# A row of 1/rms by way of HBM instead of four transposes, in a two-layer encoder trunk on one core

## The chip, the core and the metric

One core of one Trainium2 chip. The metric is the device time of one execution in microseconds (us), lower is better. Engines go by the profile's names: PE (TensorE, matmuls), PEld (its weight loads), DVE (VectorE), ACT (ScalarE), POOL (GpSimd) and SP (SyncE, which here only issues DMAs).

## The reference

Two layers over one sequence of 512 tokens of width 1024, all in float32. In short:

```python
xn = rmsnorm(x, norm1_g)
u, q, k, v, g_a, g_b = split(xn @ w_in)          # u, v, g_a, g_b: 1024 wide; q, k: 4 heads x 2 x 128
q, k = rotary(rmsnorm(q)), rotary(rmsnorm(k))    # per head, first 32 of 128 entries turned
a = softmax(q0 k0) - lam * softmax(q1 k1)        # per head, chunk-causal with chunks of 64
o = rmsnorm(a @ v) * (1 - lam_init)
p = (windowed mean of u over 2, 4, 8, 16 tokens - u) @ w_pool * pool_scale
x = x + (sigmoid(g_a) * p + sigmoid(g_b) * o) @ w_out
x = x + swiglu(rmsnorm(x, norm2_g))              # hidden width 2816
```

rmsnorm(x) is x / sqrt(mean(x^2) + 1e-6) times a gain. The 1/rms is one number per token. It can therefore be applied after a product with `w_in`, which is what the kernel does.

## The kernel before, in words

**Products.** A float32 product is made of three matmuls of rounded parts: each operand is split in a high part (a cast on ACT, the first half of `split`, L213) and a low part (the difference, a subtraction on DVE, the second half). `product` (L303) then issues ah x bh, ah x bl and al x bh (L308, L309, L310) for each slice of the inner dimension. Names end in h and l (or hi and lo): xh, xl; qh, ql; vh, vl; uh, ul; and ah, al for the probabilities.

**Weights.** They come as 307 pieces of 512 KB in the order of `weight_plan` (L61). `loaded` (L220) requests a piece on SP's queue into one of seven buffers `raw` (L225) and notes the request in the list `transfers`.

**Round trips through HBM.** SP's queue also carries the kernel's block transposes: `turned` (L318) transposes within blocks on DVE (L323), writes the tile to HBM (`away<-near`, L324) and reads it back in another order (`near<-away`, four transfers, L328). A transfer on SP's queue that must wait holds everything behind it.

**Order of the work.** `clock` counts the columns that the matmuls have taken so far (a matmul of 512 columns adds 512, a transpose 256, L316). `later(delay, what)` (L261) puts a step into a heap, due `delay` columns from now, and `run_due` (L271), called ahead of every slice of a product, issues what has fallen due. So steps are written into the program between the matmuls at places that the counter sets, and the framework's scheduler makes each engine's order of that. Every engine works its instructions in order and waits where one is not ready.

**A layer's first half.** The heads are worked in the order 3, 2, 1, 0 (`attention`, L523). For each: the product for q and k (`evicted`, `rotated`, `turn`), and per block t of 128 tokens the scores (`scores`, L548, with a mask memset L558, a maximum on DVE L559 and the exponential on ACT L560), the difference of the two softmaxes, its transpose, the split into `ah` and `al` (`turn_prob`, L577), and the product with v (`weighted`, L596), whose result ACT squares (L604). The widest scores, of the last block, have 512 columns. v itself comes from a product whose result ACT and DVE evict into vh and vl (L691, L692).

`merged(j)` (L733) follows a head by one: it makes u and the gate g_a of group j. `windowed` (L709) multiplies u by the row of 1/rms on DVE (`up`, L714), adds shifted copies (`us`, L719), and finishes with three short steps (`head`, L722, L723, L725), after which u is split into uh and ul. For the gates, DVE multiplies the product by the row of 1/rms (`ta<-mm,hg`, L748), ACT takes the tanh (L752).

**The row of 1/rms.** `token_stats` (L429) makes 1/rms with tokens along the partitions: `stats[:, 1, :]`, 128 partitions x 4, by a pow on POOL (L440). `windowed` and the gates need it with tokens along the free dimension and the same in all 128 partitions: `rms_rows[layer]`, which is the second half of the tile `hg` (`head_gains`, L176; the first half holds rotary tables). `spread_rms` (L501) makes that row: it transposes each column of `stats`, broadcast to 128 x 128, on PE (L315) into one PSUM bank, and ACT copies the bank into `hg` (L506). It is queued by `later(81600, ...)` at the layer's start (L512). Its first reader is `up` of the first head's `merged`.

Of the kernel before, what the change touches and what calls it, by code (L numbers as in the profile page):

```python
# [10 lines left out]
F32 = mybir.dt.float32  # L11
# [7 lines left out]
P = 128  # L19
# [3 lines left out]
NT = S // P  # L23
# [31 lines left out]

QK_AWAY, SCORE_AWAY, PROB_AWAY, AV_AWAY, MERGE_AWAY = 28000, 26000, 32000, 18000, 24000
NORMED, ROTATED, JOINED, GATED, SUMMED, GATE = 7200, 2400, 2400, 4800, 9600, 2400
HIDDEN_DELAYS = (26000, 28000), (8000, 14000)


# [64 lines left out]
def trunk_kernel(  # L125
# [10 lines left out]
    nc = tc.nc  # L136
# [3 lines left out]
    hbm = ctx.enter_context(tc.tile_pool(name="hbm", bufs=1, space=bass.MemoryType.DRAM))  # L140
# [29 lines left out]
    rotary, rms_rows = {}, {}  # L170
# [5 lines left out]
    def head_gains(layer):  # L176

        g = sb.tile([P, 2, S], F32, name="hg", tag="hg")
        rms_rows[layer] = g[:, 1, :]
        cs, sn = rotary[layer] = [g[:, 0, i * VD:(i + 1) * VD].rearrange("p (a t r) -> p a t r", a=2, t=NT) for i in range(2)]  # L180
        row = sb.tile([P, 2, ROT], F32, name="gr", tag="m12")
        for a in range(2):
            nc.sync.dma_start(row[:, a, :], spread(rows[layer][R_QG + QK * a:R_QG + QK * a + ROT]))
        for a in range(2):
            def times(to, table, gains):
                nc.gpsimd.tensor_tensor(to, table, gains.unsqueeze(1).broadcast_to(list(table.shape)), op=ALU.mult)
            times(cs[:, a], cos_t, row[:, a, :])
            for h in range(2):
                here, there = slice(h * HALF, (h + 1) * HALF), slice((1 - h) * HALF, (2 - h) * HALF)
                times(sn[:, a, :, here], sin_t[:, :, here], row[:, a, there])  # L190
        nc.gpsimd.tensor_tensor(gain_column(layer, 0), gain_column(layer, 0), gain_column(layer, 1), op=ALU.mult)
        nc.gpsimd.memset(gain_column(layer, 0)[:ROT], 1.0)
# [16 lines left out]
    transfers = []  # L209

    def split(hi, lo, src):

        return nc.scalar.copy(hi, src), nc.vector.tensor_sub(lo, src, hi.bitcast(F32))  # L213
# [47 lines left out]
    def later(delay, what):  # L261
        heapq.heappush(waiting, (clock[0] + delay, count[0], what))
        count[0] += 1
# [50 lines left out]
    def transpose(dst, src):  # L314
        nc.tensor.transpose(dst, src, ident)  # L315
        clock[0] += 2 * P  # L316

    def turned(src, n, tag=None, bufs=1, near=None, wait=0):  # L318

        if near is None:  # L320
            near = sb.tile([P, n * P], F32, name="near", tag=tag, bufs=bufs)
        away = hbm.tile([P, n * P], F32, name="away", tag="away", bufs=8)
        nc.vector.transpose(near.rearrange("p (c k j) -> p k c j", c=4, k=n), src.rearrange("p (k c i) -> p k c i", k=n, c=4))  # L323
        nc.sync.dma_start(away, near)  # L324

        def back():
            for c in range(4):
                nc.sync.dma_start(  # L328
                    near[32 * c:32 * (c + 1), :].rearrange("i (q r) -> i q r", q=4),
                    away.rearrange("(q i) (c r) -> c i q r", q=4, c=4)[c])  # L330

        def back_behind():
            with tc.issue_after(transfers[-1].ins):
                back()

        if wait:
            later(wait, back_behind)
        else:
            back()
        return near.rearrange("p (q k j) -> p k q j", q=4, k=n)  # L340

    def squares_of(x):
        return x.rearrange("p k (q j) -> p k q j", q=4)
# [48 lines left out]
    def token(t):  # L392
        return slice(t * P, (t + 1) * P)
# [19 lines left out]
    stats = [None]  # L413
# [86 lines left out]

    def spread_rms(layer):  # L501

        row = tr_ps()
        for t in range(NT):
            transpose(row[:, token(t)], stats[0][:, 1, t:t + 1].broadcast_to([P, P]))
        nc.scalar.copy(rms_rows[layer], row)  # L506

    for layer in range(L):
        lam_init = 0.8 - 0.6 * math.exp(-0.3 * layer)
        if layer:  # L510
            head_gains(layer)
        later(81600, lambda layer=layer: spread_rms(layer))  # L512

        def x_tok(t):
            return [(xh[:, k, token(t)], xl[:, k, token(t)]) for k in range(KD)]
# [335 lines left out]
        class Hidden:  # L851
# [9 lines left out]
            def put(self, half, t, gate, up):  # L861
# [10 lines left out]
                if t:  # L872
                    back, done = HIDDEN_DELAYS[self.f0 >= GROUPS[-1] and self.f0 < ODD]
                    near = turned(h.rearrange("p i t c -> p (i t c)"), 4, ("up", "us")[half], 2, wait=back)
                    later(back + done, lambda: self.back(half, near))

            def back(self, half, near):

                with tc.issue_after(made[0].ins), tc.issue_after(made[1].ins):
                    split(*(squares_of(x[:, half].rearrange("p i c -> p (i c)").rearrange("p (k c) -> p k c", c=P))  # L880
                            for x in self.parts), near)
                ready.add((layer, self.f0, half))
# [222 lines left out]
```

## Time and profile before

| what | value |
|---|---|
| median of 3 runs | 1377.12 us (1376.54 to 1377.54) |
| the profiled execution | 1376.3 us, of it 1374.5 us span |
| PE busy | 1369.2 us (6238 matmuls and transposes) |
| DVE busy | 996.2 us |
| ACT busy | 775.5 us |
| POOL busy | 131.2 us |
| DMA | 224.07 MB, mean 163 GB/s |

The span goes from the first to the last instruction of the profiled execution. Busy times of an engine's instructions can overlap, since its pipeline starts one before the last has ended: for PE, the distance between two starts tells more than a duration does. A row of the timeline gives the start, the duration, the engine, the line, the operation with output and inputs, the shape, a count where several like ones stand together, and in brackets how long the engine was idle before it and for whom it waited.

### The profile page before, as it was taken

The page shows a single profiled execution, that of the slowest core. Times are in us where ns is not written, and L with a number is a line of the kernel's source. Part 1 is how long each engine was busy: PE and PEld are TensorE (multiplying, and loading weights), DVE is VectorE, ACT ScalarE, POOL GpSimd, SP SyncE. Part 2 cuts the span into 40 slices and gives each one's busy share as a digit, 9 for nine tenths or more (in the row PEclk, how much of TensorE's full clock was granted, in tenths as well). Part 3 has the DMA queues.
Part 4 walks back from the last instruction along what each step waited for, and adds up shares of the span by engine and source line. Part 5 has one row for each costly group of instructions (what it writes and reads, how often), then busy time and mean ns, then how long its engine had stood idle before and what let it go on. Part 6 is the DMA issues. An engine that isn't in the chain of part 4 may idle for free.

```text
span 1374.5 us, 18657 instructions
## 1 busy us (share of the span) xinstructions
PE 1369.2 (100%) x6238; PEld 1138.2 (83%) x6238; DVE 996.2 (72%) x1787; ACT 775.5 (56%) x1577; POOL 131.2 (10%) x155
## 2 busy tenths in 40 slices
PE   9999999999999999999999999999999999999999
PEld 7888888888888888888888888888888888888887
DVE  7668667687968768678666786765878687686782
ACT  7765554554757545554367755556557665555540
POOL 4010100000101101110010001010001111000100
PEclk9999999999999999999999999999999999999999
DMA  8244444444667968676435455444536788687831
GB/s 314 86 144 133 135 139 146 146 130 147 138 179 196 234 183 213 176 202 190 143 107 165 130 171 160 138 131 139 162 111 140 197 217 214 189 207 178 206 123 62
DMA packets 141072, 224.07 MB, mean 163 GB/s; under 512 B 41392, under 2 KB 88496, under 8 KB 140976
## 3 DMA queue, kind: packets, MB, share of 16 engines
q1 hardware_dynamic: 130464, 187.20, 42.7%
q0 software_dynamic: 9216, 33.56, 14.2%
q10 hardware_dynamic: 1296, 2.13, 0.6%
q8 instruction: 49, 0.80, 0.2%
q14 instruction: 47, 0.39, 0.1%
HBM read 193.59 MB, written 29.23 MB: 162 GB/s over the span
## 4 chain that ended last, share of the span: by engine, by line
PE 99%; DMA 0%; issue 0%; DVE 0%; ACT 0%; SPq 0%; ACTq 0%; DVEq 0%
PE mm L290 17%; PE mm L289 17%; PE mm L291 17%; PE mm L308 15%; PE mm L309 15%; PE mm L310 15%; PE mm L485 0%; PE mm L484 0%; PE mm L486 0%; PE mm L315 0%; PE mm L438 0%; DMA res<-in_x_t 0%; PE mm L493 0%; ACT ah L213 0%; DVE xh L473 0%
## 5 line engine op out<-in xcount | busy, mean ns | idle before, releaser
L213 DVE TENSOR_TENSOR wlo<-raw,whi 128x1024 fp32r<-128x1024 f32 (+1 forms) x220 | 266.8, 1217 | 75.7 <-ACT whi L213 74.9
L213 ACT CAST whi<-raw 128x1024 fp32r<-128x1024 f32 (+1 forms) x220 | 229.4, 1051 | 143.4 <-PE mm L291 75.0
L308 PE MATMUL mm<-whi,xh 128*128 128x512 f32 x480 | 188.8, 393 | 0.0
L310 PE MATMUL mm<-whi,xl 128*128 128x512 f32 x480 | 187.1, 390 | 0.0
L309 PE MATMUL mm<-wlo,xh 128*128 128x512 f32 x480 | 187.1, 390 | 0.0
L289 PE MATMUL mm<-whi,xh 128*128 128x512 f32 x384 | 149.6, 390 | 0.0
L291 PE MATMUL mm<-whi,xl 128*128 128x512 f32 x384 | 149.4, 389 | 0.0
L290 PE MATMUL mm<-wlo,xh 128*128 128x512 f32 x384 | 149.4, 389 | 0.0
L290 PE MATMUL mm<-fl,whi 128*128 128x512 f32 (+1 forms) x356 | 137.6, 387 | 0.0
L291 PE MATMUL mm<-fh,wlo 128*128 128x512 f32 (+1 forms) x356 | 137.6, 387 | 0.0
L289 PE MATMUL mm<-fh,whi 128*128 128x512 f32 (+1 forms) x356 | 137.6, 387 | 0.0
L767 DVE TENSOR_TENSOR res<-mm,res 128x512 f32<-128x512 f32 (+1 forms) x145 | 97.7, 678 | 44.0 <-PE mm L291 41.8
L353 POOL TENSOR_TENSOR r<-r,mhalf 128x4 f32<-128x4 f32 (+1 forms) x64 | 59.3, 929 | 512.0 <-DVE r L352 492.1
L239 POOL DMA_DIRECT2D wlo<-in_wts x64 | 56.1, 876 | 536.6 <-ACT wlo L238 363.0
L310 PEld LDWEIGHTS mm<-whi,xl 128*128 128x128 f32 x480 | 90.1, 188 | 19.2
L309 PEld LDWEIGHTS mm<-wlo,xh 128*128 128x128 f32 x480 | 90.3, 188 | 17.3
L308 PEld LDWEIGHTS mm<-whi,xh 128*128 128x128 f32 x480 | 90.2, 188 | 17.3
L308 PE MATMUL mm<-xh,whi 128*128 128x512 f32 x256 | 99.8, 390 | 0.0
L309 PE MATMUL mm<-xl,whi 128*128 128x512 f32 x256 | 99.8, 390 | 0.0
L310 PE MATMUL mm<-xh,wlo 128*128 128x512 f32 x256 | 99.6, 389 | 0.0
L291 PEld LDWEIGHTS mm<-whi,xl 128*128 128x128 f32 x384 | 72.1, 188 | 15.0
L290 PEld LDWEIGHTS mm<-wlo,xh 128*128 128x128 f32 x384 | 72.1, 188 | 15.0
(220 smaller groups left out, 2761.9 us busy)
## 6 DMA issues: line engine op xcount, KB each, us to landing
raw<-in_wts SPq DMA_DIRECT2D x243, 512.0 KB, 3.9
wlo<-in_wts POOLq DMA_DIRECT2D x64, 512.0 KB, 6.2
away<-near SPq DMA_DIRECT2D x73, 256.0 KB, 2.3
near<-away SPq DMA_DIRECT2D x292, 64.0 KB, 2.8
away<-near SPq DMA_DIRECT2D x29, 128.0 KB, 1.9
near<-away SPq DMA_DIRECT2D x116, 32.0 KB, 2.1
pwr<-in_pool_w ACTq DMA_DIRECT2D x8, 256.0 KB, 2.9
out<-res SPq DMA_DIRECT2D x7, 256.0 KB, 2.0
```

The source lines that it names most:

```text
L213: return nc.scalar.copy(hi, src), nc.vector.tensor_sub(lo, src, hi.bitcast(F32))
L239: nc.gpsimd.dma_start(lo.rearrange("p a b -> p (a b)"), wts[piece_no], accum_op=ALU.add)
L289: nc.tensor.matmul(acc, lhsT=ah, rhs=bh, start=start, stop=False, **check)
L290: nc.tensor.matmul(acc, lhsT=ah, rhs=bl, start=False, stop=False, **check)
L291: last = nc.tensor.matmul(acc, lhsT=al, rhs=bh, start=False, stop=stop, **check)
L308: nc.tensor.matmul(acc, lhsT=ah, rhs=bh, start=i == 0, stop=False)
L309: nc.tensor.matmul(acc, lhsT=ah, rhs=bl, start=False, stop=False)
L310: last = nc.tensor.matmul(acc, lhsT=al, rhs=bh, start=False, stop=i == n - 1)
L353: nc.gpsimd.tensor_tensor(r, r, mhalf[:, :width], op=ALU.pow)
L767: return nc.vector.tensor_add(res[d][:, cs], acc, res[d][:, cs])
```

## The change

`spread_rms` no longer uses PE and ACT. It takes a small buffer `row` in HBM (4 x 128 numbers), writes `stats[:, 1, :]` into it with one transfer on SP's queue (128 partitions x 4 numbers of 4 bytes, turned by the pattern of the destination), and queues a second transfer 36000 columns later, which reads the 512 numbers back, broadcast to 128 partitions, into `hg`. The second is tied in the program's order behind the newest request of weights (`transfers[-1]`). The first step is queued for 72000 columns instead of 81600. The four calls of `transpose` no longer add their 4 x 256 columns to `clock`.

```diff
+ROW_BACK = 36000
...
     def spread_rms(layer):
 
-        row = tr_ps()
-        for t in range(NT):
-            transpose(row[:, token(t)], stats[0][:, 1, t:t + 1].broadcast_to([P, P]))
-        nc.scalar.copy(rms_rows[layer], row)
+        row = hbm.tile([NT, P], F32, name="row", tag="row", bufs=2)
+        nc.sync.dma_start(row.rearrange("t p -> p t"), stats[0][:, 1, :])
+
+        def back():
+          with tc.issue_after(transfers[-1].ins):
+            nc.sync.dma_start(rms_rows[layer], row.rearrange("t p -> (t p)").partition_broadcast(P))
+
+        later(ROW_BACK, back)
 
     for layer in range(L):
...
-        later(81600, lambda layer=layer: spread_rms(layer))
+        later(72000, lambda layer=layer: spread_rms(layer))
```

In the rows that follow, line numbers of after are one higher up to `spread_rms` and five higher behind it, and buffer numbers differ; the tiles named before and after are the same ones.

SP's queue in layer 0, before: the first weights, two rows of parameters (`lv`), and the weights behind them.

```order
L225 DMA raw<-in_wts 128x1024 x4
L686 DMA lv<-in_rows 128x512 x2
L225 DMA raw<-in_wts 128x1024 x13
L324 DMA away<-near 128x512
L328 DMA near<-away 32x4x128 x4
```

The same place after.

```order
L226 DMA raw<-in_wts 128x1024 x4
L691 DMA lv<-in_rows 128x512 x2
L505 DMA row<-stats 128x4x1
L226 DMA raw<-in_wts 128x1024 x4
L509 DMA hg<-row 128x512
L226 DMA raw<-in_wts 128x1024 x9
```

The write of the row stands ahead of 13 requests of weights and the read ahead of 9. In layer 1 the two stand next to each other, behind nine requests of weights and ahead of two `away<-near` and eight `near<-away`.

PE in layer 1, around the third block of `weighted` of the second head (`mm_7930<-vh,ah`) and the first gate product of `merged` for group 2 (`mm_7891<-xh,whi`; `mm_7951` is the next gate product), before.

```order
L310 MATMUL mm_7891<-xh_6424,wlo_7722 128x512
L308 MATMUL mm_7930<-vh_7437,ah_7841 128x256
L309 MATMUL mm_7930<-vl_7438,ah_7841 128x256
L308 MATMUL mm_7951<-xh_6424,whi_7703 128x512
L309 MATMUL mm_7951<-xl_6425,whi_7703 128x512
L310 MATMUL mm_7951<-xh_6424,wlo_7704 128x512
L310 MATMUL mm_7930<-vh_7437,al_7842 128x256
```

The same place after (`mm_7885` is the gate product, `mm_7924` the block).

```order
L309 MATMUL mm_7885<-xh_6421,whi_7715 128x512
L310 MATMUL mm_7885<-xl_6422,whi_7715 128x512
L311 MATMUL mm_7885<-xh_6421,wlo_7716 128x512
L309 MATMUL mm_7924<-vh_7431,ah_7835 128x256
L310 MATMUL mm_7924<-vl_7432,ah_7835 128x256
L311 MATMUL mm_7924<-vh_7431,al_7836 128x256
```

The three matmuls of the next gate product no longer stand between the block's second and third matmul.

DVE at that place, before: the last steps of the window (`us`, `head`), the low part `al` of the block's probabilities, and `ta`, the gate product times the row.

```order
L719 TENSOR_TENSOR us_7884<-us_7881 128x512
L213 TENSOR_TENSOR al_7842<-pr_7641,ah_7841 128x384
L722 TENSOR_TENSOR head_7887<-us_7884,tab_68 128x16
L723 SCALAR_TENSOR_TENSOR us_7884<-us_7884,up_7872 128x496
L725 TENSOR_TENSOR us_7884<-head_7887,up_7872 128x16
L748 TENSOR_TENSOR ta_7949<-mm_7891,hg_6559 128x512
```

The same place after.

```order
L724 TENSOR_TENSOR us_7875<-us_7872 128x512
L753 TENSOR_TENSOR ta_7943<-mm_7885,hg_6556 128x512
L723 MEMSET us_7878 128x16
L724 TENSOR_TENSOR us_7878<-us_7875 128x512
L718 MEMSET up_8729 128x16
L727 TENSOR_TENSOR head_7881<-us_7878,tab_68 128x16
L728 SCALAR_TENSOR_TENSOR us_7878<-us_7878,up_7866 128x496
L730 TENSOR_TENSOR us_7878<-head_7881,up_7866 128x16
L723 MEMSET us_8732 128x16
L718 MEMSET up_8778 128x16
L214 TENSOR_TENSOR al_7836<-pr_7635,ah_7835 128x384
```

`ta` has moved ahead of the window's last step, and `al` behind all of the window. On ACT the cast of that block's `ah`, which stood ahead of the tanh of `ta` with two instructions between them, now stands directly behind it.

## The prediction

> **What bounds the kernel now.** I read the page first, then the list of waits on PE, then the timelines of the places that the change touches.
>
> ```profile
> span 1374.5 us, 18657 instructions
> PE 1369.2 (100%) x6238; PEld 1138.2 (83%) x6238; DVE 996.2 (72%) x1787; ACT 775.5 (56%) x1577; POOL 131.2 (10%) x155
> PE 99%; DMA 0%; issue 0%; DVE 0%; ACT 0%; SPq 0%; ACTq 0%; DVEq 0%
> ```
>
> ```profile
> PE mm L405 <- DVE us L718: 1.2, 1, 1.2
> PE mm L493 <- DVE xh L473: 0.6, 1, 0.6
> ```
>
> The third line is the chain that ended last: 99% of it is PE. The list of PE's waits has two rows, both at the start, 1.8 us in all. So there is one bound from end to end, and only two kinds of effect count: instructions that PE no longer has to do, and new moments in which PE has nothing it may start. The profiled execution took 1376.3 us (span 1374.5), 0.8 under the median of 1377.12, so I add the change's sum to both alike. A measurement of this kernel can tell about 0.2%, 2.75 us, from no change.
>
> **What it removes.** Per layer four transposes of the 1/rms column on PE and one copy on ACT.
>
> ```profile
> 53.10 0.60 PE L315 MATMUL mm<-ident,stats 128*128 128x128 f32 x4
> 53.45 0.42 PE L308 MATMUL mm<-qh 128*128 128x384 f32 x1
> ```
>
> ```profile
> 727.61 0.60 PE L315 MATMUL mm<-ident,stats 128*128 128x128 f32 x4
> 727.96 0.48 PE L308 MATMUL mm<-whi,xh 128*128 128x512 f32 x1
> 728.27 0.39 PE L309 MATMUL mm<-wlo,xh 128*128 128x512 f32 x1
> ```
>
> ```profile
> 729.86 0.57 ACT L506 COPY hg<-mm 128x512 f32<-128x512 f32 x1
> ```
>
> Durations of pipelined matmuls overlap, so I go by starts. The four transposes hold PE for 53.45 - 53.10 = 0.35 us, and again 0.35 in layer 1; the matmul behind them is followed after 0.31 (727.96 to 728.27), where two 512-column matmuls follow each other by 0.22 or 0.23 (807.20 and 807.42 further down), so another 0.08, which I take for layer 0 as well. That is 0.43 a layer, **-0.87 us** in all. The copy (0.57) goes from an engine that is 56% busy and is not on the chain: 0.
>
> **What it adds on SP.** Two transfers per layer, `row<-stats` and `hg<-row`, in the queue that carries the weights and the round trips. The first can't leave before POOL's pow has made 1/rms, the second not before the first has landed, and all that stands behind them on SP waits too.
>
> ```profile
> 22.43 2.01 POOL L440 TENSOR_TENSOR stats<-stats,mhalf 128x4 f32<-128x4 f32 x1
> ```
>
> ```profile
> 16.00 12.03 SPq L225 DMA_DIRECT2D raw<-in_wts  x7
> ```
>
> ```profile
> 30.66 2.01 ACT L213 CAST whi<-raw 128x1024 fp32r<-128x1024 f32 x2
> 33.64 0.47 ACT L691 ACTIVATE vh<-mm,stats 128x256 fp32r<-128x256 f32 x1 [0.97 <-PE mm L310]
> ```
>
> ```profile
> raw<-in_wts SPq DMA_DIRECT2D x243, 512.0 KB, 3.9
> near<-away SPq DMA_DIRECT2D x116, 32.0 KB, 2.1
> ```
>
> Layer 0: before, the weights behind `lv` were requested from 16.00 on. Now they stand behind `row`, which waits for the pow's end at 24.44: about 8.5 us later. They take 3.9 to land, so they are there at about 29, and the casts that read them stand at 30.66; ACT then still idles 0.97. Cover 1.5 us or more, cost 0. If it were gone, each microsecond would first eat that 0.97 of ACT.
>
> ```profile
> 693.35 0.33 SPq L225 DMA_DIRECT2D raw<-in_wts  x1
> 707.55 1.84 SPq L324 DMA_DIRECT2D away<-near  x2
> ```
>
> ```profile
> 702.02 1.04 POOL L440 TENSOR_TENSOR stats<-stats,mhalf 128x4 f32<-128x4 f32 x1 [54.49 <-DVE stats L439]
> ```
>
> ```profile
> 719.34 0.69 DVE L213 TENSOR_TENSOR ql<-near,qh 128x512 fp32r<-128x512 f32 x1 [1.80 <-ACT qh L213]
> ```
>
> ```profile
> 726.85 0.33 PE L308 MATMUL mm<-qh 128*128 128x256 f32 x1
> ```
>
> Layer 1: nothing stands between the two new transfers, so the delay of 36000 units that the code puts between them does not separate them in SP's queue. But SP has nothing to do from 693.68 to 707.55. `row` leaves when the pow ends at 703.06; the round trips are due at 707.55, 4.5 us later; and what they feed (`ql`, ready at 720.03) is wanted by PE at 726.85, another 6.8. Less some 0.9 for two issues, `row` may take 10.4 us to land before PE notices. The trace has no transfer of 512 pieces of 4 bytes. Below, it is bounded by a small round trip's 2.1 us; above, by four times that, 8.4, if pieces alone count (that transfer has 128 of them). Both lie under 10.4: cost 0, with the upper end as a rival below.
>
> **What it moves.** The four transposes advanced the counter of columns by 1024 units a layer, and everything queued by that counter now falls due at slightly other places; the orders in the section on the change show where this bites: layer 1, second head, third block of `weighted`. Before, that block's ah and al were cast early, the cast of `al` stood ahead of the window's last steps on DVE, and PE had three matmuls of the next gate product between the block's second and third matmul. After, the block comes directly behind the last matmul of the first gate product; on DVE `ta`, which waits for that matmul, stands ahead of a whole tail of the window and of `al`; on ACT the tanh of `ta` stands ahead of `ah`. So PE waits for a chain that begins with its own last result.
>
> ```profile
> 807.20 0.39 PE L310 MATMUL mm<-xh,wlo 128*128 128x512 f32 x1
> 807.42 0.28 PE L308 MATMUL mm<-vh,ah 128*128 128x256 f32 x1
> 807.54 0.28 PE L309 MATMUL mm<-vl,ah 128*128 128x256 f32 x1
> ```
>
> ```profile
> 793.41 0.11 DVE L558 MEMSET mm<- 64x64 f32 x1 [0.67 <-PE mm L310]
> 806.02 0.67 DVE L719 TENSOR_TENSOR us<-us 128x512 f32<-128x512 f32 x1
> 806.75 0.67 DVE L719 TENSOR_TENSOR us<-us 128x512 f32<-128x512 f32 x1
> 807.34 0.55 DVE L213 TENSOR_TENSOR al<-pr,ah 128x384 fp32r<-128x384 f32 x1
> 807.81 0.17 DVE L722 TENSOR_TENSOR head<-us,tab 128x16 f32<-128x16 f32 x1
> 808.57 0.68 DVE L748 TENSOR_TENSOR ta<-mm,hg 128x512 f32<-128x512 f32 x1
> ```
>
> ```profile
> 802.77 0.62 ACT L213 CAST uh<-us 128x512 fp32r<-128x512 f32 x1 [1.50 <-DVE us L725]
> 803.29 0.51 ACT L213 CAST ah<-pr 128x384 fp32r<-128x384 f32 x1
> 809.75 0.62 ACT L752 ACTIVATE ta<-ta 128x512 f32<-128x512 f32 x1
> ```
>
> In the clock of this trace, with PE 0.43 ahead in layer 1: PE would take the block at 807.42 - 0.43 = 806.99. `ta` can start when the gate product is out, 807.20 + 0.39 - 0.43 = 807.16, if DVE is free. But DVE works without a gap from 793.41, where the widest scores of the head start it, and those now come six 512-column matmuls later: 6 x 0.23 - 0.43 = 0.95 later. The step behind which `ta` now stands gave way at 806.75; with 0.95 that is **807.70**, which I take. Then: `ta` until 808.38 (0.68), tanh, and the cast of `ah` 0.52 behind it (802.77 to 803.29), done after 0.51: 809.41. PE has been idle for 2.4. Two matmuls 0.12 apart bring it to 809.65. On DVE behind `ta` stand one more `us` (0.59, 806.75 to 807.34), three short steps (0.76, 807.81 to 808.57), some 0.2 of memsets, and `al` (0.55): 808.38 + 2.1 = 810.48. The third matmul starts there instead of at 807.23: **+3.2 us**, in two parts, 2.4 and 0.8. With a free DVE it is 2.7; with the gaps between dependent steps that I have not counted, 3.7.
>
> ```profile
> 813.74 0.39 PE L310 MATMUL mm<-xh,wlo 128*128 128x512 f32 x1
> 814.21 0.38 PE L308 MATMUL mm<-vh,ah 128*128 128x256 f32 x1
> ```
>
> What comes next on PE gains by it: the last block of the head started 0.47 behind its neighbour where 0.23 is usual, because its cast was late. With PE 3 us later, that cast is in time: **-0.24**.
>
> ```profile
> 730.32 0.62 ACT L213 CAST qh<-near 128x512 fp32r<-128x512 f32 x1
> 730.98 0.69 DVE L213 TENSOR_TENSOR ql<-near,qh 128x512 fp32r<-128x512 f32 x1
> 731.04 0.46 ACT L691 ACTIVATE vh<-mm,stats 128x256 fp32r<-128x256 f32 x1
> ```
>
> A second, smaller place: in layer 1's first head the third block's scores now come nine matmuls (9 x 0.23 = 2.07 us) behind the product that `vh` evicts, and ACT and DVE have to do `vh`, `qh` and `ql` in that time: 0.46 + 0.62 + 0.69 = 1.77. It fits by 0.3 unless DVE is held up just then: 0 to 0.3, I take **0.1**. I found no other place where the new order leaves PE without work.
>
> Sum: -0.87 + 3.2 - 0.24 + 0.1 = **+2.2 us**: 1378.5 for the profiled execution, 1379.3 for the median.
>
> **Rivals.** (A) The wait does not cost what the order says, because DVE and ACT reach the casts sooner than I reckon or PE's later work makes up for it; then only the saving is left: 1377.12 - 0.87 = 1376.2. For it: nothing in the list of waits has ever cost PE anything after 6 us. Against it: `ta` reads the very matmul behind which PE stops, and no filler is left; nothing PE loses on a 99% chain comes back. Chance 0.08.
>
> (B) Slower: the pause lets TensorE's clock fall. It decides if the pause is long enough for that; the place is the block at 807.
>
> ```profile
> 1.19 3.19 PE L405 MATMUL mm<-cold 128*128 128x512 bf16 x8 [1.19 <-DVE us L718]
> ```
>
> In the only stretch of this trace that starts from rest, eight 512-column matmuls take 3.19 us, 0.40 each, where 0.23 is usual. One such stretch behind the pause costs 3.19 x (1 - 0.23/0.40) = 1.4 us: 1379.3 + 1.4 = 1380.7, slower than before by 0.26%. For it: 3.2 us of pause is as long as that whole stretch. Against it: two matmuls lie in between, and the larger part is 2.4. Chance 0.12. The Trainium skill ("TensorE: Matmul & The Clock Gate", the table on why this matters for kernels) allows no idle gaps of PE above about 3 us, and puts the window at about 3.4 us. By that rule 2.4 and 0.8 would pass and 3.7 in one piece would not; no row here shows a pause of either length behind warm work.
>
> (C) Slower by much: the 4-byte pieces hold SP. It decides from the 10.4 us above, and each microsecond past it is one of PE's, in layer 1 surely: if `row` landed 20 us after its issue, 9.6 more, 1389. For it: 512 pieces in one transfer is a kind that this trace lacks; against it: 2 KB in all, and 8.4 us by proportion. Chance 0.04. The Trainium skill ("DMA: Bandwidth & Descriptors", rules for kernel authors) warns that a strided last dimension costs one descriptor an element, and that a plain transfer with a rearranged pattern takes 19 times a hardware transpose; 19 x 2.1 would be some 40 us, and the time about 1409.
>
> **How the numbers follow.** The forecast has the other 0.76. Its own range is 2.7 to 3.7 for the wait and 0 to 0.3 at the second place, 1378.7 to 1380.0, and with the half microsecond by which runs of before differ 1378.3 to 1380.4. To leave out no more than 2 in 10 I reach down halfway to A, 1377.4, and up to B with its scatter, 1380.9. Faster by over 0.2% (below 1374.37) needs more than all of the saving: 0.03. Slower (above 1379.87) is B, C and the top sixth of the forecast: 0.12 + 0.04 + 0.13 = 0.29. The rest, 0.68, is within 0.2%.
>
> **What would show it.** Right: no L315 rows of `ident,stats`; PE's wait list has a row for the cast of `ah` of about 2.4 and one for `al` of about 0.8 us near 807 to 810, and nothing else new; SP's two new transfers leave at about 24.5 and 703 without a later wait for weights or `ql`. Wrong: no such rows (A), matmuls 0.40 apart behind them or a PEclk below 9 (B), PE waiting for `ql` near 727 or for `whi` near 31 (C). The whole is wrong if the time falls below 1377.4 or rises above 1380.9.

## The result, and the profile after

| kernel | median us | against before |
|---|---|---|
| before | 1377.16 (1376.54 to 1377.54) | |
| after | 1391.36 (1389.80 to 1392.77) | ratio 1.0105, 95% interval 1.0093 to 1.0116 |

The change costs 14.2 us, 1.05%. The forecast was 1379.3 in a range of 1377.4 to 1380.9: the direction was right, the size was not. The profiled execution of after took 1391.62 us, its span is 1389.8. First the page of after: its span, the engines, the chain that ended last.

```profile
span 1389.8 us, 18652 instructions
PE 1376.4 (99%) x6230; PEld 1141.0 (82%) x6230; DVE 995.6 (72%) x1787; ACT 773.4 (56%) x1575; POOL 129.4 (9%) x155
PE 90%; DVE 3%; DMA 3%; ACT 2%; issue 1%; POOL 1%; SPq 1%; DVEq 0%; ACTq 0%; POOLq 0%
```

PE's part of the chain fell from 99% to 90%; DMA, DVE, ACT and POOL hold the rest. That is the sign of a stretch in which PE no longer sets the pace. PE's list of waits, which had two rows before, says for whom it stands:

```profile
PE mm L309 <- ACT qh L214: 2.4, 1, 2.4
PE mm L309 <- ACT ah L214: 2.1, 1, 2.1
PE mm L406 <- DVE us L723: 1.2, 1, 1.2
PE mm L309 <- ACT pr L565: 1.1, 2, 0.8
PE mm L316 <- ACT lam L204: 1.1, 1, 1.1
PE mm L311 <- DVE al L214: 0.7, 1, 0.7
PE mm L494 <- DVE xh L474: 0.6, 1, 0.6
PE mm L310 <- DVE ql L214: 0.6, 1, 0.6
PE mm L311 <- DVE a L214: 0.2, 1, 0.2
```

The rows of `ah` (2.1) and `al` (0.7) are the wait that the prediction announced. `lam` and `pr` belong to layer 0 (46 and 58 us), `qh`, `ql` and `a` to layer 1 (742 to 785 us): these it did not have. SP's timeline shows where they start. In layer 0:

```profile
26.67 0.38 SPq L505 DMA_DIRECT2D row<-stats  x1
27.09 1.94 SPq L226 DMA_DIRECT2D raw<-in_wts  x4
36.15 0.33 SPq L509 DMA_DIRECT2D hg<-row  x1
```

The landing times of those four requests of weights (a row of the DMA view for the window 26.9 to 29.5), and ACT's cast that reads the first of them:

```profile
DMA to landing us min/median/max: 12.9/14.3/15.6
```

```profile
40.12 1.05 ACT L214 CAST whi<-raw 128x1024 fp32r<-128x1024 f32 x1 [7.17 <-DMA raw<-in_wts]
```

The weights were requested right behind the write, at 27.1, with no wait of SP in between, and yet took 13 to 16 us to land. ACT stood idle for 7.17 us before the cast, where the prediction had counted a cover of 1.5 and then 0.97 of idle time. Behind the start, PE's first wait stands at 46 us. In layer 1:

```profile
708.27 0.38 SPq L505 DMA_DIRECT2D row<-stats  x1
716.77 0.33 SPq L509 DMA_DIRECT2D hg<-row  x1
717.19 0.86 SPq L325 DMA_DIRECT2D away<-near  x2
722.55 4.32 SPq L329 DMA_DIRECT2D near<-away  x8
```

The two kinds of new transfer on the page (count, size, median us from issue to landing), and the landing of the `away<-near` at 717:

```profile
hg<-row SPq DMA_DIRECT2D x2, 256.0 KB, 7.0
row<-stats SPq DMA_DIRECT2D x2, 2.0 KB, 8.9
```

```profile
DMA to landing us min/median/max: 5.3/5.4/5.5
```

A write of 2 KB takes 9.4 us in layer 0 and 8.5 in layer 1. SP stands still from 708.65 to 716.77; then `away<-near`, which took 2.0 here before, takes 5.4. By then the write has landed. What is under way ahead of `away<-near` is the read `hg<-row`, which is issued at 716.77 and lands 5.0 us later. The pow stands at 707.21 here and stood at 702.02 before, 5.2 later, so `near<-away` would have been due at 709.55 + 5.2 = 714.75; it goes out at 722.55, 7.8 us late.

At the matmul for which the prediction reckoned its slack (726.85 before), nothing is lost all the same: `ql` is ready at 729.78 + 0.69 = 730.47, and PE takes the scores 1.56 us later, without a wait. The losses come behind it, at 742, at 767, and most of all before the second block's scores of the second head:

```profile
729.78 0.69 DVE L214 TENSOR_TENSOR ql<-near,qh 128x512 fp32r<-128x512 f32 x1 [1.22 <-ACT qh L214]
```

```profile
732.03 0.33 PE L309 MATMUL mm<-qh 128*128 128x256 f32 x1
```

```profile
784.78 0.58 PE L309 MATMUL mm<-qh 128*128 128x256 f32 x1 [2.36 <-ACT qh L214]
```

PE at the place that the prediction spoke of, some 11 us later than it stood before:

```profile
818.17 0.39 PE L311 MATMUL mm<-xh,wlo 128*128 128x512 f32 x1
820.70 0.39 PE L309 MATMUL mm<-vh,ah 128*128 128x256 f32 x1 [2.14 <-ACT ah L214]
...
821.93 0.39 PE L311 MATMUL mm<-vh,al 128*128 128x256 f32 x1 [0.73 <-DVE al L214]
...
823.34 0.63 PE L309 MATMUL mm<-xh,whi 128*128 128x512 f32 x1
823.76 0.63 PE L310 MATMUL mm<-xl,whi 128*128 128x512 f32 x1
```

Against the usual distance of starts (0.23 and 0.12) PE loses 2.30 before `ah` and 0.89 before `al`: 3.19, where 3.2 was forecast. Behind it come five matmuls 0.43 apart: the trace grants PE half its clock from 822.26 to 825.67, and did so before from 784.71 to 788.12, behind the wait for `qh`.

### The profile page after: what moved, and what is told of

Read it like the earlier page. It is cut to its first block, busy times and chain, and to the rows that moved or that the text cites. A ratio compares the mean times of both kernels' runs of the same rounds, so it can differ in the third digit from the quotient of the medians.

```text
span 1389.8 us, 18652 instructions
## 1 busy us (share of the span) xinstructions
PE 1376.4 (99%) x6230; PEld 1141.0 (82%) x6230; DVE 995.6 (72%) x1787; ACT 773.4 (56%) x1575; POOL 129.4 (9%) x155
## 2 busy tenths in 40 slices
DMA packets 142416, 224.60 MB, mean 162 GB/s; under 512 B 42480, under 2 KB 89584, under 8 KB 142320
## 4 chain that ended last, share of the span: by engine, by line
PE 90%; DVE 3%; DMA 3%; ACT 2%; issue 1%; POOL 1%; SPq 1%; DVEq 0%; ACTq 0%; POOLq 0%
PE mm L291 17%; PE mm L292 17%; PE mm L290 17%; PE mm L309 12%; PE mm L310 12%; PE mm L311 12%; DMA raw<-in_wts 1%; DMA near<-away 1%; DMA away<-near 1%; SPq L329 1%; POOL r L354 1%; DVE wlo L214 0%; ACT whi L214 0%; DVE near L324 0%; ACT qn L648 0%
```

## The experiments

**Two causes, crossed.** The change does two things that can be parted: it sends transfers, and it no longer advances the counter. Of the four combinations after is one; three kernels are the others, or nearly. Theory 1: the write of 512 pieces of 4 bytes is most of the loss. Theory 2, the rival: the new order is.

Transfers, with the counter of before:

```diff
         later(72000, lambda layer=layer: spread_rms(layer))
+        later(81600, lambda: clock.__setitem__(0, clock[0] + 8 * P))
```

> After's two transfers per layer, but the counter of columns is advanced by 1024 at 81600 as the four transposes did, so that PE, DVE and ACT keep nearly the order of before (ta of the second head stands behind al again). Theory 1 (the write of 512 pieces of 4 bytes holds SP's queue and all that is behind it for some 9 us, and that is most of the loss): after stands 14.2 above before, the order's wait at 818 us is 3.2 and the slow matmuls behind it about 1.0 of that, so about 1387 us (1384 to 1389). Theory 2 (the new order is most of the loss): only the saving is left, about 1376.3.

Measured: 1387.05 (1385.45 to 1387.35), ratio 1.0068 (1.0054 to 1.0082). As theory 1 has it.

No transfers, with the order of after:

```diff
-        row = hbm.tile([NT, P], F32, name="row", tag="row", bufs=2)
-        nc.sync.dma_start(row.rearrange("t p -> p t"), stats[0][:, 1, :])
...
+        nc.gpsimd.memset(rms_rows[layer], 1.0)
```

> No transposes and no transfers: the row is filled with ones by POOL instead, so 1/rms is left out of the pooled branch and of the gates. The counter is that of after, and PE, DVE and ACT stand in the order of after, instruction for instruction. Theory 1: this is the case that the prediction reckoned, with SP left alone: 1379.3, up to 1380.7 if matmuls go slower behind the pause, with waits on PE of about 2.4 and 0.8 near 806 to 810 us. Theory 2: about 1390.

Measured: 1381.41 (1380.12 to 1382.28), ratio 1.0030 (1.0019 to 1.0042). Nearer to theory 1, but 2.1 above the forecast that it was made to try, and 0.7 above the 1380.7 that was allowed for slow matmuls. Its timeline of PE, which begins with a wait that the forecast did not have:

```profile
776.15 0.39 PE L310 MATMUL mm<-ql,qh 128*128 128x256 f32 x1 [0.34 <-DVE ql L214]
...
807.65 0.39 PE L311 MATMUL mm<-xh,wlo 128*128 128x512 f32 x1
810.17 0.39 PE L309 MATMUL mm<-vh,ah 128*128 128x256 f32 x1 [2.14 <-ACT ah L214]
...
811.40 0.39 PE L311 MATMUL mm<-vh,al 128*128 128x256 f32 x1 [0.72 <-DVE al L214]
...
812.33 0.63 PE L309 MATMUL mm<-xh,whi 128*128 128x512 f32 x1
812.76 0.63 PE L310 MATMUL mm<-xl,whi 128*128 128x512 f32 x1
...
815.74 0.39 PE L311 MATMUL mm<-xh,wlo 128*128 128x512 f32 x1
```

The wait that was forecast is there with no transfer in the program, 2.30 + 0.88, at the time and of the size that the prediction worked out (2.4 and 0.8). From 812.33 to 815.74 eight matmuls take 3.41 us instead of 1.8, at half the granted clock: 1.6 us that the forecast held to be a rival.

Neither transfers nor the order of after:

```diff
-        row = tr_ps()
-        for t in range(NT):
-            transpose(row[:, token(t)], stats[0][:, 1, t:t + 1].broadcast_to([P, P]))
-        nc.scalar.copy(rms_rows[layer], row)
+        nc.gpsimd.memset(rms_rows[layer], 1.0)
+        clock[0] += 8 * P
```

> No transposes and no transfers, the row filled with ones by POOL (1/rms left out there), and the counter advanced by 1024 as in before. Both theories: only the saving of the transposes, 0.87 us, so about 1376.3; no wait on PE near 807. If it is faster than that by more than 0.5, the transposes cost more than their rows show.

Measured: 1377.88 (1377.31 to 1378.42), ratio 1.0006 (0.9997 to 1.0015). A miss: the saving is not seen. PE's waits tell why:

```profile
PE mm L308 <- ACT qh L213: 0.7, 1, 0.7
PE mm L309 <- DVE ql L213: 0.3, 1, 0.3
```

The scheduler orders by its own reckoning too, and without the transposes it places a few instructions of layer 1 differently even with the counter kept. At 775.7 the second block's scores of the second head then come too early for `qh` and `ql`: PE loses 0.81 + 0.61, more than the 0.87 that it saves.

The four together, medians in us (before: 1377.1 beside them):

| | counter kept | counter of after | the order costs |
|---|---|---|---|
| no transfers | 1377.88 | 1381.41 | 3.5 |
| transfers | 1387.05 | 1391.36 | 4.3 |
| the transfers cost | 9.2 | 10.0 | |

Both theories name a real cost; the transfers' is 9 to 10 us, the order's 3.5 to 4.3. The intervals of these kernels are 1.2 to 1.9 us wide to either side, so within them the two costs add up. The kernels of one column have the same order on PE, DVE and ACT, but that of the left column isn't before's: it has the 0.81 + 0.61 just told.

Since after and the kernel without transfers have one order, each matmul's start can be compared in the two traces. After is 1.7 us behind at 15 us (the start, of which more below), 5.1 at 345 and still 5.1 at 735 us, 10.5 at 790 and 10.5 at 1370 us (times of the kernel without transfers). So the transfers cost 3.4 us in layer 0 and 5.4 in layer 1, the latter between 742 and 786 us of after.

**What about the transfers costs so much.** The number of pieces, first: the same write with each partition's four numbers side by side.

```diff
-        row = hbm.tile([NT, P], F32, name="row", tag="row", bufs=2)
-        nc.sync.dma_start(row.rearrange("t p -> p t"), stats[0][:, 1, :])
+        row = hbm.tile([P, NT], F32, name="row", tag="row", bufs=2)
+        nc.sync.dma_start(row, stats[0][:, 1, :])
...
-            nc.sync.dma_start(rms_rows[layer], row.rearrange("t p -> (t p)").partition_broadcast(P))
+            nc.sync.dma_start(rms_rows[layer], row.rearrange("p t -> (p t)").partition_broadcast(P))
```

> After, but the write goes out as 128 pieces of 16 bytes (each partition's four numbers side by side), so the row comes back with its tokens permuted; orders on all engines and the place in SP's queue are those of after. If the number of pieces sets the write's 8.9 us: landing in about 2 to 3 us, and a time near that of the kernel without transfers, 1379.5 to 1383 (the broadcast read stays). If the wait is there for another reason (a small write just takes that long, or the place in the queue): about 1391 as after.

Measured: 1381.78 (1379.98 to 1382.62), ratio 1.0032 (1.0020 to 1.0045). The write's landing:

```profile
row<-stats SPq DMA_DIRECT2D x2, 2.0 KB, 1.4
```

The same bytes from the same place in the program's order: 1.4 us instead of 8.9, and the time is that of the kernel without transfers (1381.41) within the noise. The profile's count of DMA packets falls from 142416 to 141648, by twice the 384 pieces that are fewer in each layer. So all but 0.4 of the 10 us hangs on the pieces. The broadcast read costs nothing that shows here, where it goes out 3.1 us ahead of layer 1's `away<-near` (704.97 and 708.04, landing in 2.0); in after it stood right ahead of them, because the write held it up. PE waits as long as in the kernel without transfers, but in this execution the clock holds (0.23 between the starts that follow):

```profile
812.76 0.39 PE L309 MATMUL mm<-xh,whi 128*128 128x512 f32 x1
812.99 0.39 PE L310 MATMUL mm<-xl,whi 128*128 128x512 f32 x1
```

Then a size between, 256 pieces of 8 bytes:

```diff
+        row = hbm.tile([2, P, 2], F32, name="row", tag="row", bufs=2)
+        nc.sync.dma_start(row.rearrange("a p b -> p a b"), stats[0][:, 1, :].rearrange("p (a b) -> p a b", a=2))
```

> After with the write as 256 pieces of 8 bytes (the row comes back with its tokens permuted); orders are after's. 128 pieces of 16 bytes landed in 1.4 us, 512 of 4 bytes in 8.9. If pieces cost alike from the first on: 1.4 + 128 x 7.5/384 = 3.9 us, and a time of 1382 to 1385. If 4 bytes are a special case: about 1.5 us and 1381.8. If two bytes-per-piece steps cost alike: up to 5.

Measured: 1381.27 (1379.50 to 1383.20), ratio 1.0029 (1.0018 to 1.0041), and this landing:

```profile
row<-stats SPq DMA_DIRECT2D x2, 2.0 KB, 3.4
```

The landing grows with the pieces from the first on (1.4, 3.4, 8.9), a little faster than in proportion. The time was expected at 1382 to 1385 and stays at 1381.3: 3.4 us are within the slack in both layers, 8.9 are not.

**In which layer, and by which way.** The change in layer 0 alone:

```diff
+        if layer != 0:
+            row = tr_ps()
...
+            return
```

> The change in layer 0 alone; layer 1 keeps its transposes, and the counter is advanced as before, so that the order is that of before but for one place in layer 0. After's trace puts PE's waits in layer 0 at 46.5 (1.3), 58 (0.9), 60 (0.5) and 78 us (0.3), 3.0 in sum, and it saves 0.43. Theory 1: 1377.1 + 2.6 = 1379.7, the other 7 of the transfer's cost being layer 1's. Theory 2 (all of the loss comes from layer 1's round trips, and layer 0's waits are the start's slow clock): 1376.7.

Measured: 1380.70 (1380.41 to 1381.60), ratio 1.0026 (1.0017 to 1.0035): 3.5 us above before, where theory 1 said 2.6. PE's waits are those of after in layer 0, with 1.0 for `ah` at 76 us and 0.4 for `al` behind it in addition.

The write alone, added to before, with nothing taken away:

```diff
+    def write_row():
+
+        row = hbm.tile([NT, P], F32, name="row", tag="row", bufs=2)
+        nc.sync.dma_start(row.rearrange("t p -> p t"), stats[0][:, 1, :])
...
         later(81600, lambda layer=layer: spread_rms(layer))
+        later(72000, write_row)
```

> Before with nothing taken away and the write alone added in both layers, at 72000, on SP's queue; nobody reads it. PE, DVE, ACT and POOL stand exactly in the order of before. Theory 1 (the write by itself is the larger part of the loss): layer 0 costs the 3.9 us of the kernel with layer 0 alone, and with layer 1's round trips 5 us late the time is 1384 to 1387. Theory 2 (the loss needs the new order, or SP standing still before the read): 1377 to 1379.

Measured: 1382.29 (1381.61 to 1383.73), ratio 1.0039 (1.0026 to 1.0053): 5.3 us for 2 x 2 KB that nobody reads. Between the two theories' ranges, and PE's waits show why:

```profile
PE mm L308 <- ACT pr L566: 1.3, 2, 1.0
PE mm L315 <- ACT lam L203: 1.3, 1, 1.3
...
PE mm L308 <- ACT hg L506: 0.8, 1, 0.8
PE mm L309 <- DVE ql L213: 0.3, 1, 0.3
...
```

All but the row of `ql` lie in layer 0. In layer 1 `near<-away` still goes out 5.0 us late, but the slack takes that: 0.5 is lost at 781. So the write by itself harms layer 0; in layer 1 it needs help. To the 9.2 of both transfers with the counter kept 3.9 are missing. Two things are different there: the read, for which SP stands still for 8 us until the write has landed, and the order, which here is before's and there is one that puts the second head's scores too early. No run parts the two.

To take SP's standing still away, the read was queued later:

```diff
-ROW_BACK = 36000
+ROW_BACK = 100000
```

> After with the read queued 100000 columns behind the write instead of 36000, so that SP no longer stands still before the read until the write has landed; the write stays where it is, and layer 1's order differs somewhat from after's. If SP's standing still is the cost: about 1382, as with the transfers left out. If the write itself keeps what is behind it in the queue from moving: layer 0's weights again land 13 us after their request, layer 1's round trips again 5 us or more after theirs, and the time stays at 1387 to 1391.

Measured: 1385.94 (1384.38 to 1387.58), ratio 1.0062 (1.0050 to 1.0075): 5.4 below after, far from 1382, and 1.1 below the lower end of the other forecast. The weights of layer 0 take 13.1 to 17.5 us to land, as expected of a write that holds up what is behind it. In layer 1 `away<-near` goes out on time but lands after 5.9 to 7.1 us, here with the write itself under way. `near<-away` is 5.1 us late instead of 7.8, and PE still loses 3.3 before the second block's scores of the second head, as much as in after (2.5 + 0.6). So SP's standing still isn't needed for that loss. With the write added to before the same lateness, 5.0, cost 0.5: that speaks for the new order as the help that the write needs. But this kernel's order in layer 1 isn't quite after's either, so the point is argued from two kernels and not shown.

And with the write issued by POOL, on POOL's queue:

```diff
-        nc.sync.dma_start(row.rearrange("t p -> p t"), stats[0][:, 1, :])
+        nc.gpsimd.dma_start(row.rearrange("t p -> p t"), stats[0][:, 1, :])
```

> The kernel with the late read, but with the write issued by POOL, on POOL's own queue; all orders but SP's and POOL's are the same as in that kernel. If the write of 512 pieces blocks only its own queue: the weights on SP's queue land in about 4 us again, and the time is 1380 to 1382. If it holds the DMA engines for everyone: weights late as before, 1387 to 1391.

Measured: 1383.01 (1381.78 to 1384.64), ratio 1.0043 (1.0030 to 1.0055): 2.9 below its twin, and between the two forecasts. Layer 0 has no wait left. But not because the others are free: this is the landing of the three weights requested between 24 and 30 us, the first of which went out ahead of the write. In before, the two requested between 26.5 and 29 us took 3.9 to 4.2.

```profile
DMA to landing us min/median/max: 5.8/11.3/11.6
```

The write holds up transfers of another queue as well. Layer 0 is saved because its weights no longer stand behind the write: SP requests them from 16.41 on, as before. In layer 1, where `away<-near` takes up to 6.7 us, the wait before the scores is the same as in the twin:

```profile
PE mm L309 <- ACT qh L214: 2.3, 1, 2.3
...
PE mm L310 <- DVE ql L214: 0.6, 1, 0.6
```

**Can the row be had without loss?** With 16 bytes to a piece, and DVE reading the row in the order in which it lies:

```diff
+    def by_rms(to, x, layer):
+        to, x = (v.rearrange("q (t p) -> q t p", t=NT) for v in (to, x))
+        nc.vector.tensor_mul(to, x, rms_rows[layer].rearrange("q (p t) -> q t p", t=NT))
```

> After with the write as 128 pieces of 16 bytes and the row kept with its tokens permuted; the multiplications on DVE that read it take it in that order, 16 bytes apart (eight per layer for the windows' products and eight for the gates), so that the whole computation is done. Orders are after's. If DVE reads such a row as fast as one in order: as the kernel with wide pieces, 1381.8. If it is slower, L719 and L753 take more than 0.68 us, and a DVE that is 95% busy around 800 us adds that to the wait at 807: up to 1384.

Measured: 1382.96 (1382.39 to 1383.54), ratio 1.0041 (1.0028 to 1.0053). The second case: the products with the row (L753 in after, L515 here; busy, mean ns of one) become slower by half, and the wait for `ah` grows from 2.30 to 3.36.

```profile
L753 DVE TENSOR_TENSOR ta<-mm,hg 128x512 f32<-128x512 f32 x16 | 10.9, 684 | 4.3 <-PE mm L311 4.3
```

```profile
L515 DVE TENSOR_TENSOR ta<-mm,hg 128x512 f32<-128x512 f32 x16 | 17.0, 1060 | 2.9 <-PE mm L311 2.8
```

With POOL's queue, in the layer that bears it:

```diff
+        if layer:
+            row = tr_ps()
...
+            return
...
+        nc.gpsimd.dma_start(row.rearrange("t p -> p t"), stats[0][:, 1, :])
```

> The change in layer 0 alone, with the write on POOL's queue and the read queued 100000 columns behind it; layer 1 keeps its transposes; the order on PE is that of before without the four transposes of layer 0. If the write's harm in layer 0 is that weights stand behind it in the queue: no waits there, 1377.1 - 0.4 = 1376.7, which can't be told from before. If it holds up the weights from another queue as well: 1379 to 1380.7.

Measured: 1376.34 (1376.02 to 1376.63) beside 1376.95 for before, ratio 0.9995 (0.9986 to 1.0004). It is the lowest median of all, but the interval holds 1: what it brings, half of the saving or so, can't be told from no change. PE's waits are the two at the start:

```profile
PE mm L406 <- DVE us L731: 1.2, 1, 1.2
PE mm L494 <- DVE xh L474: 0.4, 1, 0.4
```

**The start.** In every profile but that of before, PE ran slowly in its first ten microseconds. The kernel before once more:

> The kernel before, unchanged, for a second profile of it. Every profile but the first one of before has PE's warm-up of eight matmuls at 3.5 to 3.6 us instead of 3.19 and is 0.9 to 2.5 us later by the tenth microsecond. If that comes by chance: the warm-up here takes 3.5 to 3.6 and the span is about 1 us longer, and none of the loss belongs to the change. If the change brings it: 3.19 and 1374.5 as in the first profile.

Measured: 1377.04, ratio 1.0000 (0.9991 to 1.0009), span 1375.3, and a start as in all the others:

```profile
1.18 3.59 PE L406 MATMUL mm<-cold 128*128 128x512 bf16 x8 [1.18 <-DVE us L719]
```

It comes by chance; the profile that the prediction was made from had the lucky start. In it the trace's record of the full clock begins at 3.8 us, here at 7.1, and in after at 9.9. Spans are compared with this 1375.3 below.

## Why the prediction was wrong, step by step

**The saving, -0.87: right.** The transposes are gone. In the kernel with layer 0 alone on POOL's queue, PE was 0.34 late against before ahead of the place of the transposes (53 us) and 0.10 early behind it: 0.44, where 0.43 was forecast for a layer.

**Layer 0, cost 0: wrong.** The step was "they take 3.9 to land, so they are there at about 29". 3.9 is the median of 243 requests over the whole kernel. At this place it was not the usual one even in before, where the three requested at 16.0 to 17.3 took 7.6 to 8.8. With the wide pieces the first three behind the write took 5.2 to 7.2, and the cover held (no wait of PE there). Behind the write of 512 pieces it was 12.9 to 15.6, and the first cast came at 40.12. The cover had to be taken with the new neighbour in the queue. Alone, the change in layer 0 made the kernel 3.5 us slower.

**Layer 1, cost 0: wrong in what the slack was taken to cover, not in the landing.** The upper bound for the write, 8.4 by the count of pieces, was good: 8.5 in this layer. The sum let nothing but SP wait, and left out that `away<-near` would take 5.4 instead of 2.0. The point from which the write hurts, 10.4, was reckoned for one place, the scores at 726.85, and there the cover held by 1.56. The failed step is to let it stand for the whole layer. The head's last scores had less: in before `ql` was ready for them at 731.67 and wanted at 737.57, 5.9 instead of 6.8. At the second block's scores of the second head the new order had left nothing at all (0.61 lost without transfers). Against the kernel of the same order without transfers, PE lost 1.0 at 742, 0.8 at 767, and 3.6 at 782 to 786, where it also ran at half clock for a while: 5.4 in all. The write alone is almost borne there in before's order (0.5). How the 5.4 divide between the order, the read and SP's standing still stays open.

**Rival (C), chance 0.04:** its cause, the 4-byte pieces, is what happened, but not by its condition. The landing stayed under 10.4 (8.5), and the loss came in layer 0, where the prediction did not look for it, and in layer 1 behind the place that it looked at. The time of 1391.4 is near its 1389, which was worked out for a landing of 20 us; that is luck. The rule of the Trainium skill ("DMA: Bandwidth & Descriptors", rules for kernel authors) that a strided last dimension means one descriptor an element points the right way, and the trace agrees: 512 pieces 8.9 us, 128 pieces 1.4, and a DMA packet for every piece. The factor of 19 on the same page, from which the prediction estimated 40 us, is not seen here.

**The wait at 807, +3.2: right**, in place, chain and size: 2.30 + 0.88 with no transfers in the program. DVE's `ta` started at 808.37 there, 0.33 us after PE's last matmul ended (808.04): DVE was the late one, as reckoned.

**The stall at 814, -0.24: right.** It is gone from after.

**The second place, 0.1, and "I found no other place": wrong.** The first head showed nothing without transfers; the second block's scores of the second head, at 775 to 776, lost 0.61 in the kernels with after's order and no long write.

**Rival (B), the clock, chance 0.12: real, and by chance.** Behind the pause of 2.3 and 0.9 us the granted clock fell to half in the profiles of after, of the order-only kernel and of 256 pieces, and held with the wide pieces. The six executions with 256 pieces show the same chance: the mean granted clock was 1.000 in two (1379.5 and 1379.6 us) and 0.998 in four (1381.2 to 1383.2). The estimate for it was 1.4 us; it cost 1.6 in the order-only kernel. The Trainium skill ("TensorE: Matmul & The Clock Gate", the table on why this matters) sets the limit at gaps of about 3 us; the trace does not agree: in these three the longest single gap was 2.14, and two matmuls lay between it and the next, of 0.7.

**The sum without the transfers** then closes: -0.87 + 0.61 + 3.19 + 1.6 - 0.24 = 4.3, and the spans differ by 1379.6 - 1375.3 = 4.3. The forecast of 2.2 lacked the 0.6 and the 1.6. With the transfers, after's span is 14.5 above the 1375.3: the same 4.3, 3.4 in layer 0, 5.4 in layer 1 with the slow clock there, and 1.7 of a still slower start. That makes 14.8; the two programs' ends differ by the 0.3 that is too much.

## What to carry to other kernels

Price a small transfer by its pieces, not by its bytes, and look at what its neighbours' landing becomes, in its queue and in others: the median landing of a queue that flows is no cover for what comes right behind such a write. Taking instructions off the busiest engine also changes what a counter or a scheduler makes of the rest; read the new order for places where an engine waits for a chain that starts with its own last result, since those can be worked out to a tenth of a microsecond. A slack covers the place for which it was worked out: here it held there, and the time was lost at later places that had less.

## What the runs showed of the hardware

- A write of 2 KB from 128 partitions landed in 1.4 us as 128 pieces of 16 bytes, in 3.4 as 256 of 8, and in 8.5 to 11.0 as 512 of 4. While the last was under way, 512 KB of weights on SP's queue took 12.9 to 15.6 us, and up to 11.6 where the write was on POOL's queue; two requested there in before took 3.9 to 4.2.
- In layer 1, a read of 256 KB, broadcast to 128 partitions, landed in 5.0 us; two transfers of 256 KB issued right behind it took 5.4 instead of 2.0, and 2.0 where it went out 3.1 us ahead of them.
- Behind a pause of PE of 2.3 and 0.9 us with two matmuls between, the granted clock fell to 0.5 in some executions: 512-column matmuls start 0.43 apart for 3.41 us, beginning 0.3 to 0.9 us after the pause's end. In another execution with the same pause it held.
- DVE's product of a row in PSUM with a row whose elements lie 16 bytes apart took 1060 ns instead of 684.
- PE's first ten microseconds vary by chance: eight matmuls in 3.19 to 3.60 us, the first record of the full clock at 3.8 to 9.9 us, and up to 2.5 us lost until the tenth.
